# Another order of work in a state-space mixer: quarter-array inputs, transposes over the outputs' bank, weight groups held to ready tiles

## The chip, the cores and the metric

The kernel runs on one core of a Trainium2 chip. Its engines work side by side, each through its own instructions in order: TensorE (PE) multiplies matrices, VectorE (DVE) and ScalarE (ACT) do elementwise work, GpSimd (POOL) does some more and starts DMAs, and SyncE's queue (SP) starts most of the DMAs. The metric is the device time of one execution, in microseconds (us); lower is better.

## The reference, cut to what matters

The program is one step of a decoder with two layers. Layer 0 mixes tokens with a short convolution, layer 1 with a complex diagonal state-space model and a gated output. Each layer ends in a squared-ReLU MLP. There are 272 prompt positions and 32 sample positions, held as 304 columns (four interleaved rows of 76), and 2048 features, which are 16 tiles of 128.

```python
def s5_mixer(u, h0_re, h0_im, ...):          # layer 1; 128 groups of 16 channels, 64 complex states each
    abar, bbar = discretise(lam, log_step, b)
    bu = einsum('btgc,gpc->btgp', u32, bbar)               # inputs of the states
    h = scan(h_t = abar * h_{t-1} + bu_t)                  # over positions, with the initial state h0
    y = einsum(c, h) + d_skip * u32
    g = gelu(y)
    return (g @ w_a) * sigmoid(g @ w_b)                    # 2048 x 2048 each
...
h = h + mixer(rmsnorm(h)); h = h + sq_relu_mlp(rmsnorm(h), w_up, w_down)    # 2048 -> 8192 -> 2048
```

## The kernel before, in words

**Weights and slots.** Every weight matrix is read as pieces of 256 rows by 512 columns (512 KB), one piece to a *slot*. ACT rounds a piece to its high half `whi` (L67), DVE subtracts to get the low half `wlo` (L69), and PE makes 24 products per slot (L200 to L202: high by high, high by low, low by high, for four blocks of 128 outputs and two feature tiles). `take()` of slot i prepares the halves of slot i+2 and starts DMAs some slots further ahead. Halves lie in three buffers, so the halves of slot i+2 need slot i-1 to be finished. A *group* is a run of slots that sum into four PSUM banks of seven that go round; the next group's fourth bank is the first of the group before, so it must have been read by then.

**Layer 0's MLP and the work behind it.** Up groups (8 slots) and down groups (4 slots each, four in a row) alternate. Results of an up group are taken out one per slot during the next group, in a chain across DVE and ACT: `zt` (L919), `at` (L921), high half on ACT (L814), low half on DVE (L815). Results of a down group are added to `h` (L876). Meanwhile a list `bg` of small jobs computes the mixer's matrices (powers of the decay, input and output matrices, rotations); after every slot the next job, or the next piece of a job that contains `yield`, is emitted. The jobs that the change touches are `t_a4` and `t_a4b` (transposes on PE and copies on DVE), `t_m2` (output matrices: a product, a second product, their sum, on DVE, L680 to L683) and `t_rot` (rotation tables).

**The mixer.** For each of the 16 feature tiles t:

- `st_m1` (L1036): the inputs of the states, from `ssm["U"]` by a matrix `m1` that DMAs load from DRAM. A tile's two halves of 64 channels stand as blocks on the diagonal of a 128 x 128 matrix whose other blocks are zero, written once by `G.memset` and then left. Two matrices are held. The result lies in PSUM banks 4 and 5 (`xbank`).
- `st_scan` (L1064 to L1076) on DVE: two products by the rotation and their sum, `scale_u` (L1180) for tile t+2, the scan (L1069), two products back, the states `S` and the last state. On ACT `st_samples` (L1051, L1052) copies the sample columns and `rho_fill` (L1056) writes decays.
- `st_t` (L1098) and `st_y` (L1108) on PE: outputs from the inputs and from the states, in half arrays, into banks 6 and 7 (`ybank`); ACT copies them out (L1114).
- `st_c(t)`: PE transposes the outputs (L1121) into `cbank`, unused columns of banks 4 and 5; ACT does the gelu (L1123) and the high half of `g` (L1125); the low half, `lo()` (L1128), runs on DVE.

**What fills the PE between them.** The gated output's weights are multiplied as early as `g` allows: `EARLY` lists groups and how many feature tiles each takes before the loop ends (partial sums are copied out by ACT, L1209, and added later), `LATE` lists what is left. `PERSTEP[t]` says how many slots step t may emit, half of them at `between(1)`, the rest at `between(2)`, and `run_slots` emits a slot only when the tiles that it needs are past `lo()`. In steps 0 and 1 ten matmuls of ones by ones (`warm`, L1225) follow `st_t`. The order of every engine is the order in which this code runs; nothing reorders it.

**Names of steps used below.** "Step t" is one pass of the loop over tiles. y(t) stands for the output matmuls L1108 of tile t, m1(t) for its input matmuls.

Of the kernel before, what the change touches and what calls it, by code (L numbers as in the profile page):

```python
# [31 lines left out]
WARM = 10  # L32
ULAG = 2
WP = 12
# [46 lines left out]
def build(ctx, tc, I, O, dbg=None):  # L81
# [369 lines left out]
    def prep_tasks():  # L451
# [112 lines left out]
        def t_a4():  # L564
# [38 lines left out]
        def t_a4b():  # L603
            ps = psum1()
            for x, n in enumerate((27, 0, 1)):
                T.transpose(out=ps[:64, x * P:(x + 1) * P], in_=nat(n), identity=ident)
            for g2 in range(2):
# [61 lines left out]
        def t_m2(ri, hf, i):  # L669
# [12 lines left out]
            V.tensor_tensor(out=tmp, in0=c[1 - ri], in1=a[1], op=ALU.mult)  # L682
            V.tensor_tensor(out=o, in0=o, in1=tmp, op=ALU.add if ri == 0 else ALU.subtract)  # L683
# [105 lines left out]
        L += [None] * 12  # L789
        for c in range(8):  # L790
            L.append(lambda c=c: t_kmm(c))
            if c < 6:
                L.append(lambda c=c: t_kload(c + 2))
            L += [lambda c=c: t_rot(c), lambda c=c: t_rotout(c)]
# [157 lines left out]
    def ssm_alloc():  # L952
# [3 lines left out]
        ssm["m1"] = [xr[:, i * 1024:(i + 1) * 1024].rearrange("p (n m) -> p n m", m=P) for i in range(2)]  # L956
        ssm["m2"] = [xr[:, 2048 + i * 512:2560 + i * 512].rearrange("p (n m) -> p n m", m=64) for i in range(2)]
        ssm["tt"] = [xr[:, 3072 + i * 256:3328 + i * 256].rearrange("p (n m) -> p n m", m=64) for i in range(2)]
        ssm["rot"] = [xr[:, 3584 + i * 816:3584 + (i + 1) * 816] for i in range(3)]
        ssm["tmp"] = [xr[:, 6032 + i * 544:6032 + (i + 1) * 544] for i in range(3)]  # L960
        ssm["yt"] = [xr[:NK, 7664 + i * 512:8176 + i * 512] for i in range(2)]
        sel = ssm["sel"] = xr[:, 8688:9200].rearrange("p (j m) -> p j m", j=4)
# [9 lines left out]
        G.memset(xr[:, 0:2048], 0.0)  # L972
# [5 lines left out]
        for t in range(2):  # L978
            load_m1(t)
            load_rot(t)  # L980
        load_rot(2)
        for t in range(2):
            load_t(t)
            load_m2(t)
        ssm["h0"] = b[:, 0:1024].rearrange("p (r a x) -> p r a x", r=2, a=4)
# [24 lines left out]
    def load_m1(t):  # L1010
        for g2, g in enumerate(HALF):
            nc.sync.dma_start(out=ssm["m1"][t % 2][g, :, g], in_=d_m1[t, g2].rearrange("x q r p -> x (q r) p"))

    def load_m2(t):
        nc.sync.dma_start(out=ssm["m2"][t % 2], in_=d_m2[t].rearrange("g x q r p -> (g x) (q r) p"))
# [9 lines left out]
    xbank = banks[:, 2048:3072].rearrange("p (q x) -> p q x", q=4)  # L1025
    xst = xbank[:, :, 0:2 * NK].rearrange("p q (r k) -> p q r k", r=2)
    ybank = [banks[:NK, 3072 + g * 512:3328 + g * 512] for g in range(2)]
    cbank = xbank[:, :, 2 * NK:3 * NK]
    GBANK = (0, 1, 2, 3)

    def st_m1(t):

        m = ssm["m1"][t % 2]
# [4 lines left out]
        if t + 2 < NT:  # L1038
            load_m1(t + 2)
# [8 lines left out]
    def st_samples(t):  # L1048

        qs = slice(t * 4, t * 4 + 4)  # L1050
        S.activation(out=ssm["F0"][:, 1:9, :, qs].rearrange("p s r q -> p q r s"), in_=xst[:, :, :, NP:NK], func=AF.Copy)  # L1051
# [7 lines left out]
    def st_scan(t, between):  # L1059
# [3 lines left out]
        x = xst[:, :, :, 0:NP]  # L1063
        V.tensor_tensor(out=v3(a), in0=x, in1=co, op=ALU.mult)  # L1064
        V.tensor_tensor(out=v3(b), in0=x[:, :, ::-1], in1=si, op=ALU.mult)
        between(0)
        V.tensor_tensor(out=a, in0=a, in1=b, op=ALU.add)
        between(1)
        V.tensor_tensor_scan(out=b, data0=ssm["rho"][t % 2], data1=a, initial=0.0, op0=ALU.mult, op1=ALU.add)  # L1069
        between(2)  # L1070
        V.tensor_tensor(out=v3(a), in0=v3(b), in1=co, op=ALU.mult)
        V.tensor_tensor(out=v3(c), in0=v3(b)[:, :, ::-1], in1=si, op=ALU.mult)
        between(3)
# [29 lines left out]
    def st_y(t):  # L1103

        for n in range(8):
            q, r = n // 2, n % 2
            for g2, g in enumerate(HALF):
                T.matmul(out=ybank[g2][:, q * 64:(q + 1) * 64], lhsT=ssm["S"][t % 2][g, q, r, :], rhs=ssm["m2"][t % 2][g, n, :],  # L1108
                         start=False, stop=n == 7)
        if t + 2 < NT:  # L1110
            load_m2(t + 2)
# [27 lines left out]
    def warm_sqrt():  # L1139
        w = tp.tile([P, 1], F32, tag="warm", name="warm")  # L1140
        S.activation(out=w, in_=one1, func=AF.Sqrt)
# [4 lines left out]
    def ssm_pre(t):  # L1146
        def sa():
# [4 lines left out]
            if t == 5:  # L1152
                warm_sqrt()
# [10 lines left out]
    flush()  # L1164
    u_in(8, NT)
# [7 lines left out]
    rsqrt_from(ps[:, :NK], rstd2[:, NK:2 * NK], rstd2[:, 2 * NK:3 * NK], rT)  # L1173
    for f in h0_copies:
        f()
# [14 lines left out]
    def early():  # L1190

        for (n, mg), c in EARLY:
# [7 lines left out]
            for si in range(0, c, 2):  # L1200
                yield si + 2
                hi, lo = W.take()
                for m, kk in slot_order(si, si + 2 >= c):
                    mm(m, kk, si, hi, lo)
            for i in range(4):
                if (n, mg) in pslot:
                    a = pslot[n, mg] * 4 + i
# [170 lines left out]
```

## Time and profile before

| what | value |
|---|---|
| median of 3 runs | 2521.21 us (2519.66 to 2521.39) |
| profiled execution | 2520.97 us, span 2519.0 us |
| PE busy | 2438.4 us, 97% of the span |
| DVE busy | 1537.7 us, 61% |
| ACT busy | 965.3 us, 38% |
| POOL busy | 134.6 us, 5% |
| the mixer | from about 1360 us of the span to about 1560 us |

The page counts busy time per engine, but matmuls are pipelined, so a busy PE is not always at full speed; the granted clock (full is 2.4 GHz, shown as 1.00; 0.50 is 1.2 GHz) has to be read beside it. A wait is put down to the semaphore that came last. Where a row shows `x16`, so many instructions that follow each other are merged, and an fp32 matmul counts as two.

### The profile page before, as it was taken

How to read it: one execution, taken by the hardware profiler on the slowest of the kernel's cores; microseconds unless marked ns; L12 is line 12 of the kernel's file. 1: busy time of each engine (PE TensorE's matmuls, PEld its weight loads, DVE VectorE, ACT ScalarE, POOL GpSimd, SP SyncE). 2: the span in 40 equal slices, each digit the busy share in tenths (PEclk: the TensorE clock that was granted, in tenths of full speed). 3: DMA queues.
4: the chain of work that ended last, by engine and by line, in shares of the span. 5: the costliest groups of instructions: out<-in, count | busy, mean ns of one | idle time of the engine just before them, and what ended most of it. 6: DMA issues, size and time to landing. Idle time of an engine off the chain costs nothing.

```text
span 2519.0 us, 44232 instructions
## 1 busy us (share of the span) xinstructions
PE 2438.4 (97%) x18526; PEld 2418.0 (96%) x18526; DVE 1537.7 (61%) x2302; ACT 965.3 (38%) x1241; POOL 134.6 (5%) x239
## 2 busy tenths in 40 slices
PE   6999999999999999999998898999999999999998
PEld 6999999999999999999998898999999999999997
DVE  5644555875657774767655776676555555545555
ACT  4333334434433333333433443453333333333334
POOL 2000000000011120000300002000000000000000
PEclk9999999999999999999998899999999999999999
DMA  6555555456676667666759663556555555555553
GB/s 153 157 159 157 157 158 178 143 150 185 162 214 174 195 189 211 195 202 208 214 161 228 167 189 121 170 165 166 165 166 167 168 161 169 165 168 167 167 165 109
DMA packets 245829, 432.39 MB, mean 172 GB/s; under 512 B 48404, under 2 KB 52180, under 8 KB 245596
## 3 DMA queue, kind: packets, MB, share of 16 engines
q1 hardware_dynamic: 236160, 396.30, 53.9%
q0 software_dynamic: 9408, 33.20, 5.3%
q8 instruction: 145, 2.38, 0.4%
q14 instruction: 56, 0.46, 0.1%
q10 hardware_dynamic: 60, 0.05, 0.0%
HBM read 400.44 MB, written 29.05 MB: 171 GB/s over the span
## 4 chain that ended last, share of the span: by engine, by line
PE 51%; DMA 1%; ACT 1%; issue 0%; DVE 0%; SPq 0%; DVEq 0%; ACTq 0%
PE banks L200 16%; PE banks L202 16%; PE banks L201 16%; PE banks L1036 1%; PE banks L1108 1%; DMA d_u<-h 1%; PE banks L1098 0%; DMA ssm_xr<-d_m 0%; PE banks L1342 0%; SPq L1006 0%; ACT gt L1123 0%; PE banks L1225 0%; PE banks L1121 0%; ACT sq L324 0%; ACT ssm_big L1209 0%
## 5 line engine op out<-in xcount | busy, mean ns | idle before, releaser
L69 DVE TENSOR_TENSOR wlo<-raw,whi 128x1024 fp32r<-128x1024 f32 x704 | 864.2, 1228 | 810.7 <-ACT whi L67 809.6
L67 ACT ACTIVATE whi<-raw 128x1024 fp32r<-128x1024 f32 x704 | 742.7, 1057 | 956.0 <-PE banks L201 806.0
L200 PE MATMUL banks<-hid,whi 128*128 128x304 f32 (+1 forms) x2048 | 611.9, 299 | 15.6 <-DVE h L876 13.8
L202 PE MATMUL banks<-xs_m,wlo 128*128 128x304 f32 (+1 forms) x2048 | 611.8, 299 | 0.7 <-DVE wlo L69 0.7
L202 PE MATMUL banks<-hid,wlo 128*128 128x304 f32 (+1 forms) x2048 | 611.1, 298 | 1.3 <-DVE wlo L69 1.3
L201 PE MATMUL banks<-hid,whi 128*128 128x304 f32 (+1 forms) x2048 | 611.7, 299 | 0.0
L201 PE MATMUL banks<-xs_m,whi 128*128 128x304 f32 (+1 forms) x2048 | 611.0, 298 | 0.0
L200 PE MATMUL banks<-xs_m,whi 128*128 128x304 f32 (+1 forms) x2048 | 610.8, 298 | 0.0
L200 PEld LDWEIGHTS banks<-hid,whi 128*128 128x128 f32 x2048 | 385.7, 188 | 17.8 <-DVE h L876 15.3
L202 PEld LDWEIGHTS banks<-hid,wlo 128*128 128x128 f32 x2048 | 386.5, 189 | 2.1 <-DVE wlo L69 2.1
L202 PEld LDWEIGHTS banks<-xs_m,wlo 128*128 128x128 f32 x2048 | 385.4, 188 | 1.6 <-DVE wlo L69 1.6
L200 PEld LDWEIGHTS banks<-xs_m,whi 128*128 128x128 f32 x2048 | 385.3, 188 | 1.3 <-issue 0.4
L201 PEld LDWEIGHTS banks<-hid,whi 128*128 128x128 f32 x2048 | 385.8, 188 | 0.0
L201 PEld LDWEIGHTS banks<-xs_m,whi 128*128 128x128 f32 x2048 | 385.3, 188 | 0.1
L200 PE MATMUL banks<-xs,whi 128*128 128x304 f32 x768 | 233.6, 304 | 3.6 <-DVE h L391 3.6
L202 PE MATMUL banks<-xs,wlo 128*128 128x304 f32 x768 | 233.3, 304 | 0.0
L201 PE MATMUL banks<-xs,whi 128*128 128x304 f32 x768 | 232.6, 303 | 0.0
L814 ACT ACTIVATE hid<-at 128x304 fp32r<-128x304 f32 (+1 forms) x128 | 57.8, 452 | 302.2 <-DVE at L921 302.2
L200 PE MATMUL banks<-g,whi 128*128 128x288 f32 x512 | 154.8, 302 | 0.7 <-ACT g L1125 0.7
L201 PE MATMUL banks<-g,whi 128*128 128x288 f32 x512 | 151.9, 297 | 0.9 <-DVE g L1128 0.9
L202 PE MATMUL banks<-g,wlo 128*128 128x288 f32 x512 | 151.7, 296 | 0.0
L200 PEld LDWEIGHTS banks<-xs,whi 128*128 128x128 f32 x768 | 145.8, 190 | 3.9 <-DVE h L391 3.8
(260 smaller groups left out, 2304.3 us busy)
## 6 DMA issues: line engine op xcount, KB each, us to landing
raw<-in_mlp_w_up SPq DMA_DIRECT2D x256, 512.0 KB, 3.8
raw<-in_mlp_w_down SPq DMA_DIRECT2D x256, 512.0 KB, 3.8
raw<-in_conv_w_in SPq DMA_DIRECT2D x96, 512.0 KB, 3.8
raw<-in_conv_w_out SPq DMA_DIRECT2D x32, 512.0 KB, 3.7
raw<-in_ssm_glu_w_a SPq DMA_DIRECT2D x32, 512.0 KB, 3.7
raw<-in_ssm_glu_w_b SPq DMA_DIRECT2D x32, 512.0 KB, 4.2
d_rot<-prep POOLq DMA_DIRECT2D x8, 816.0 KB, 4.3
ssm_xr<-d_rot SPq DMA_DIRECT2D x16, 408.0 KB, 4.7
```

The lines of the kernel that those rows point to most:

```text
L67: self.nc.scalar.activation(out=hi, in_=r, func=AF.Copy)
L69: eng.tensor_tensor(out=lo, in0=r, in1=hi.bitcast(F32), op=ALU.subtract)
L200: T.matmul(out=o, lhsT=wh, rhs=xh, start=si == 0 and kk == 0, stop=False)
L201: T.matmul(out=o, lhsT=wh, rhs=xl, start=False, stop=False)
L202: T.matmul(out=o, lhsT=wl, rhs=xh, start=False, stop=si + 2 >= len(kts) and kk == 1)
L814: S.activation(out=dh, in_=src, func=AF.Copy)
L1036: T.matmul(out=xbank[:, q, r * NK:(r + 1) * NK], lhsT=m[:, q * 2 + r, :], rhs=ssm["U"][:, t * 4 + q, :], start=True, stop=True)
L1108: T.matmul(out=ybank[g2][:, q * 64:(q + 1) * 64], lhsT=ssm["S"][t % 2][g, q, r, :], rhs=ssm["m2"][t % 2][g, n, :], start=False, stop=n == 7)
```

## The change

1. **Inputs by quarters of the array.** `m1` matrices are held as 128 x 64 (the two diagonal blocks below each other), four buffers instead of two, one DMA each instead of two. `st_m1` issues for each of 8 outputs two matmuls, of rows and columns 0 to 63 and of rows and columns 64 to 127. The zero fill is gone. Tile 1's inputs go to banks 2 and 3 and tiles 0, 2 and later to banks 4 and 5, so that tiles 0 and 1 are issued before the loop. `m2` has three buffers instead of two.
2. **Transposes over the outputs' accumulator.** `cbank` is now bank 6, the first of the two that `st_t` and `st_y` sum into.
3. **Order of a step.** `PERSTEP` holds two numbers: slots before `st_c(t-1)` and slots after the scan. `st_samples` comes after the transposes and the gelu of the tile before, `st_m1(t+1)` at `between(0)`, `st_t` at the end of the step. Before the second slots, `W.prep_to` prepares halves ahead of `lo()`.
4. **Gated groups.** `EARLY` starts with b0 and holds 18 slots; `LATE` ends with a whole group a3 of 8 slots. The first late group (7 slots) is emitted by the same generator as the early ones, with the same test on ready tiles. Its slots are ordered so that the earlier of two feature tiles goes first.
5. **Warm-up and tables.** `warm` is gone except for six matmuls in step 1; seven come before the sum of squares, fifteen instead of twelve after it; the activation table for gelu is loaded before the loop.
6. **Background jobs.** `t_a4` issues its four matmuls together and yields before the copies and once more after them; `t_a4b` yields after its transposes; `t_m2` yields between its second product and the sum; the first two rotations stand in place of twelve empty entries and the others one tile earlier.

```diff
-EARLY = [(("a", 0), 2), (("b", 1), 2), (("a", 1), 2), (("b", 2), 4), (("a", 2), 6), (("b", 3), 8), (("a", 3), 10),
-         (("b", 0), 16)]
-LATE = [(n, c) for n, c in EARLY[:-1]]
-PERSTEP = (0, 0, 1, 1, 2, 2, 1, 2, 1, 2, 2, 2, 2, 2, 2, 2)
+EARLY = [(("b", 0), 2), (("a", 0), 2), (("b", 1), 2), (("a", 1), 4), (("b", 2), 6), (("a", 2), 8), (("b", 3), 12)]
+LATE = EARLY + [(("a", 3), 0)]
+PERSTEP = ((0, 0), (0, 0), (0, 1), (1, 1), (1, 1), (1, 1), (0, 1), (1, 1), (1, 1), (1, 1), (1, 1), (1, 0), (0, 1),
+           (1, 1), (1, 1), (1, 0))
...
             for x in range(4):
+                T.matmul(out=ps[32 * x:32 * x + 16, 256:256 + P], lhsT=nat(30, 16), rhs=ident, start=True, stop=True)
+            yield
+            for x in range(4):
                 sl = slice(32 * x, 32 * x + 16)
-                T.matmul(out=ps[sl, 256:256 + P], lhsT=nat(30, 16), rhs=ident, start=True, stop=True)
...
             V.tensor_tensor(out=tmp, in0=c[1 - ri], in1=a[1], op=ALU.mult)
+            yield
             V.tensor_tensor(out=o, in0=o, in1=tmp, op=ALU.add if ri == 0 else ALU.subtract)
...
-    xbank = banks[:, 2048:3072].rearrange("p (q x) -> p q x", q=4)
-    cbank = xbank[:, :, 2 * NK:3 * NK]
+    xbank = [banks[:, o:o + 1024].rearrange("p (q x) -> p q x", q=4) for o in (2048, 1024)]
+    cbank = banks[:, 3072:3072 + N0].rearrange("p (i k) -> p i k", i=4)
...
         for q in range(4):
             for r in range(2):
-                T.matmul(out=xbank[:, q, r * NK:(r + 1) * NK], lhsT=m[:, q * 2 + r, :], rhs=ssm["U"][:, t * 4 + q, :],
-                         start=True, stop=True)
+                for g in HALF:
+                    T.matmul(out=x[g, q, r, :], lhsT=m[g, q * 2 + r, :], rhs=ssm["U"][g, t * 4 + q, :],
+                             start=True, stop=True)
...
     for t in range(NT):
-        n = PERSTEP[t]
+        na, nb = PERSTEP[t]
+        run_slots(na)
+        low = st_c(t - 1) if t else None
         def between(k):
             if k == 0:
-                st_samples(t)
-            elif k == 1:
                 if t + 2 < NT:
                     scale_u(t + 2)
-                k = run_slots((n + 1) // 2)
-                if t > 2:
-                    lows.append(st_c(t - 1))
-                if t + 1 < NT:
+                if t == 0:
+                    st_m1(2)
+                elif 1 < t < NT - 1:
                     st_m1(t + 1)
-                st_t(t)
-                warm(WARM if t < 2 else 0)
-            elif k == 2:
-                run_slots(n // 2)
+            else:
+                W.prep_to(W.idx + nb * (LOOK + 1))
+                if low:
+                    low()
+                run_slots(nb)
         st_scan(t, between)
+        st_t(t)
+        if t == 1:
+            warm_pe0(6)
         st_y(t)
+    run_slots(1)
+    low = st_c(NT - 1)
+    run_slots(1)
+    low()
+    run_slots(9)
```

**Where instructions move.** The first place is PE at the start of the mixer, up to the first slot. Before:

```order
L993 MATMUL banks<-ident,ssm_big 128x128 x8
L1170 MATMUL banks<-acc,ssm_xr 128x76 x4
L263 MATMUL banks<-ones 128x128 x12
L1036 MATMUL banks<-ssm_big,ssm_xr 128x76 x16
L1098 MATMUL banks<-ssm_xr,ssm_big 76x64 x8
L1225 MATMUL banks<-ones 128x128 x10
L1108 MATMUL banks<-ssm_xr,vy 76x64 x16
L1121 MATMUL banks<-ident,ssm_xr 128x76 x4
L1036 MATMUL banks<-ssm_big,ssm_xr 128x76 x8
```

Then tile 1's L1098, L1225, L1108 and L1121 follow in the same way, and the first slot. In the changed kernel the same jobs have the lines L1004, L1185, L1051 (inputs), L1112 (`st_t`), L1122 (y), L1135 (transposes) and L1239 (the six matmuls of ones):

```order
L1004 MATMUL banks<-ident,ssm_big 128x128 x8
L263 MATMUL banks<-ones 128x128 x7
L1185 MATMUL banks<-acc,ssm_xr 128x76 x4
L263 MATMUL banks<-ones 128x128 x15
L1051 MATMUL banks<-ssm_big,ssm_xr 64x76 x48
L1112 MATMUL banks<-ssm_xr,ssm_big 76x64 x8
L1122 MATMUL banks<-ssm_xr,vy 76x64 x16
L1135 MATMUL banks<-ident,ssm_xr 128x76 x4
L1112 MATMUL banks<-ssm_xr,ssm_big 76x64 x8
L1239 MATMUL banks<-ones 128x128 x6
L1122 MATMUL banks<-ssm_xr,vy 76x64 x16
```

The inputs of tiles 0, 1 and 2 (48 quarter matmuls) now stand together ahead of everything, and ten of ones are gone from each of steps 0 and 1, with six back in step 1.

The second place is ACT in one step late in the loop. Before, from y's copies (L1114) on, with the sample copies L1051 and L1052 and the gelu L1123:

```order
L1114 ACTIVATE ssm_xr<-banks 76x16x16 x2
L1051 ACTIVATE ssm_big<-banks 128x4x2x8
L1052 ACTIVATE vy<-ssm_big 128x8x8
L67 ACTIVATE whi<-raw 128x1024
L1123 ACTIVATE gt<-banks 128x288
L1125 ACTIVATE g_13689<-gt 128x288
```

In the changed kernel, with L1128 for y's copies, L1137 and L1139 for gelu and high half, L1066 and L1067 for the sample copies:

```order
L1128 ACTIVATE ssm_xr<-banks 76x16x16 x2
L67 ACTIVATE whi<-raw 128x1024
L1137 ACTIVATE gt<-banks 128x288
L1139 ACTIVATE g_13722<-gt 128x288
L1066 ACTIVATE ssm_big<-banks 128x4x2x8
L1067 ACTIVATE vy<-ssm_big 128x8x8
```

The sample copies moved from ahead of the gelu to behind it, and the inputs of the next tile (L1051 on PE), which overwrite the bank that L1066 reads, wait for L1066.

The third place is DVE in layer 0's MLP, at the end of the first down group after an up group. Before, with L680 (product), L682 and L683 (second product and sum) of the job `t_m2`:

```order
L69 TENSOR_TENSOR wlo<-raw,whi 128x1024
L919 TENSOR_TENSOR zt<-banks,rstd 128x304
L921 SCALAR_TENSOR_TENSOR at<-zt 128x304
L815 TENSOR_TENSOR hid<-at,hid 128x304
L680 TENSOR_TENSOR prep_7178<-prep_7178,nat 128x32x16
L69 TENSOR_TENSOR wlo<-raw,whi 128x1024
L682 TENSOR_TENSOR prep_7178<-prep_7178,nat 128x512
L683 TENSOR_TENSOR prep_7178<-prep_7178 128x32x16
L876 TENSOR_TENSOR h<-h,banks 128x304
```

The same rows of the changed kernel, where L928, L930, L824 and L885 are L919, L921, L815 and L876:

```order
L69 TENSOR_TENSOR wlo<-raw,whi 128x1024
L928 TENSOR_TENSOR zt<-banks,rstd 128x304
L930 SCALAR_TENSOR_TENSOR at<-zt 128x304
L824 TENSOR_TENSOR hid<-at,hid 128x304
L69 TENSOR_TENSOR wlo<-raw,whi 128x1024
L885 TENSOR_TENSOR h<-h,banks 128x304
```

In these four slots the background work on DVE went from four products and two sums, with two operations more before the first L876, to one product and one sum, with none before L885. One such down group later it is five operations (L684, L686, L688, L684, L686) in place of eight.

## Rows read from the trace of the kernel before

**Rows 1.** The page: busy time, share and instructions by engine
```profile
PE 2438.4 (97%) x18526; PEld 2418.0 (96%) x18526; DVE 1537.7 (61%) x2302; ACT 965.3 (38%) x1241; POOL 134.6 (5%) x239
```
**Rows 2.** Waits of PE up to 1345 us: total, times, longest
```profile
PE banks L572 <- DVE nat L573: 4.3, 3, 3.8
...
PE banks L202 <- DVE wlo L69: 2.0, 4, 1.0
PE banks L200 <- DVE zt L919: 1.8, 1, 1.8
```
**Rows 3.** Windows: length, busy of PE, PEld, DVE, ACT, POOL, clock, DMA, GB/s
```profile
507.00:518.00 11.00, 6.65 (x29) 4.83 (x27) 7.30 (x25) 2.35 (x3) 0.00 (x0) 0.69 0.43 105
800.00:950.00 150.00, 139.03 (x972) 137.81 (x971) 110.18 (x135) 50.60 (x56) 20.07 (x27) 0.98 0.65 195
```
**Rows 4.** Timeline of PE, layer 0's down groups: start, length, [idle before, releaser]
```profile
823.45 0.41 PE L200 MATMUL banks<-hid,whi 128*128 128x304 f32 x1 [3.94 <-DVE h L876]
...
936.32 0.41 PE L200 MATMUL banks<-hid,whi 128*128 128x304 f32 x1 [3.95 <-DVE h L876]
```
**Rows 5.** Timeline of DVE in the down group before 823 us
```profile
802.95 1.23 DVE L69 TENSOR_TENSOR wlo<-raw,whi 128x1024 fp32r<-128x1024 f32 x1 [7.05 <-ACT whi L67]
...
806.54 1.23 DVE L69 TENSOR_TENSOR wlo<-raw,whi 128x1024 fp32r<-128x1024 f32 x1 [0.47 <-ACT whi L67]
...
810.61 1.20 DVE L69 TENSOR_TENSOR wlo<-raw,whi 128x1024 fp32r<-128x1024 f32 x1
...
815.75 1.22 DVE L69 TENSOR_TENSOR wlo<-raw,whi 128x1024 fp32r<-128x1024 f32 x1
```
**Rows 6.** Chain of work that ended last, one step: start, length, work
```profile
1509.23 0.69 PE banks L1098 x16
...
1513.29 1.24 PE banks L1108 x32
...
1517.91 0.28 PE banks L1121 x4
...
1518.67 2.01 PE banks L1036 x16
```
**Rows 7.** The same chain, the mixer's start
```profile
1381.73 7.36 DMA ssm_xr<-d_m
1389.23 3.66 PE banks L1036 x16
...
1394.10 4.39 PE banks L1225 x20
...
1408.93 1.31 PE banks L1108 x32
```
**Rows 8.** Timeline of DVE, first and last operation of tile 0's scan
```profile
1369.64 0.72 DVE L1064 TENSOR_TENSOR ssm_xr<-banks,ssm_xr 128x544 f32<-128x544 f32 x1 [2.48 <-PE banks L1036]
...
1375.41 0.17 DVE L1076 TENSOR_TENSOR ssm_big<-ssm_xr 128x8 f32<-128x8 f32 x1
```
**Rows 9.** Timeline of ACT in one step of the mixer
```profile
1526.02 0.65 ACT L1114 ACTIVATE ssm_xr<-banks 76x256 f32<-76x256 f32 x2 [5.43 <-PE banks L1108]
1526.56 0.31 ACT L1051 ACTIVATE ssm_big<-banks 128x64 f32<-128x64 f32 x1
...
1526.90 1.06 ACT L67 ACTIVATE whi<-raw 128x1024 fp32r<-128x1024 f32 x1
...
1530.12 0.44 ACT L1125 ACTIVATE g<-gt 128x288 fp32r<-128x288 f32 x1
```
**Rows 10.** Chain of work, matmuls of a background job in quarter columns
```profile
1184.31 0.69 PE banks L730 x32
```
**Rows 11.** Timeline of DVE, the scan of the last tile
```profile
1541.55 2.35 DVE L1069 TENSOR_TENSOR_SCAN ssm_xr<-vy,ssm_xr 128x544 f32<-128x544 f32 x1
```
**Rows 12.** Chain of work, outputs of the last tile
```profile
1550.32 2.31 PE banks L1108 x32
```
**Rows 13.** Timeline of ACT, last copy of the 25th slot's sums
```profile
1559.88 0.41 ACT L1211 ACTIVATE vy<-banks 128x288 f32<-128x288 f32 x1 [0.39 <-PE banks L202]
```

More of the change, by code (lines that the diff above doesn't have):

```diff
@@ L1010, in load_m1 @@
     def load_m1(t):
[L1011 to L1012 removed]
+        nc.sync.dma_start(out=ssm["m1"][t % 4], in_=d_m1[t].rearrange("g x q r p -> (g x) (q r) p"))
     def load_m2(t):
[L1015 removed]
+        nc.sync.dma_start(out=ssm["m2"][t % 3], in_=d_m2[t].rearrange("g x q r p -> (g x) (q r) p"))
     def load_t(t):
@@ L1107, in st_y @@
             for g2, g in enumerate(HALF):
-                T.matmul(out=ybank[g2][:, q * 64:(q + 1) * 64], lhsT=ssm["S"][t % 2][g, q, r, :], rhs=ssm["m2"][t % 2][g, n, :],
+                T.matmul(out=ybank[g2][:, q * 64:(q + 1) * 64], lhsT=ssm["S"][t % 2][g, q, r, :], rhs=ssm["m2"][t % 3][g, n, :],
                          start=False, stop=n == 7)
-        if t + 2 < NT:
-            load_m2(t + 2)
+        if t + 3 < NT:
+            load_m2(t + 3)
         y = ssm["yt"][t % 2].rearrange("k (i q g e) -> k g i q e", i=4, q=4, g=2)
@@ L1202, in early, with warm_pe0 @@
                 hi, lo = W.take()
-                for m, kk in slot_order(si, si + 2 >= c):
+                for m, kk in [(m, kk) for m in range(4) for kk in range(2)] if c == 2 else slot_order(1, False):
                     mm(m, kk, si, hi, lo)
             for i in range(4):
-                if (n, mg) in pslot:
-                    a = pslot[n, mg] * 4 + i
-                    assert a < 16 or (a - 15) * N1 <= outs[0] * 4 * NK
-                    S.activation(out=part[:, a, :], in_=ps[i][:, :N1], func=AF.Copy)
-                else:
-                    S.activation(out=ssm["sg"][i], in_=ps[i][:, :N1], func=AF.Sigmoid)
+                a = pslot[n, mg] * 4 + i
+                assert a < 16 or (a - 15) * N1 <= outs[0] * 4 * NK
+                S.activation(out=part[:, a, :], in_=ps[i][:, :N1], func=AF.Copy)
+        kts = KALL[LATE[0][1]:]
+        for _ in range(4):
+            k = GBANK[nbank[0] % 4]
+            nbank[0] += 1
+            first.append(banks[:, k * 512:(k + 1) * 512])
+        mm = products(first, kts, rhs_g, N1)
+        for si in range(0, len(kts), 2):
+            yield kts[si] + 2
+            hi, lo = W.take()
+            for m, kk in slot_order(1, False):
+                mm(m, kk, si, hi, lo)
+    def warm_pe0(n):
+        for _ in range(n):
+            T.matmul(out=banks[:, 0:P], lhsT=ones, rhs=ones, start=True, stop=True)
     outs = [0]
+    first = []
     work = early()
@@ L1221, in run_slots @@
         return n
-    def warm(n):
-        for _ in range(n):
-            T.matmul(out=banks[:, 0:P], lhsT=ones, rhs=ones, start=True, stop=True)
     for t in range(2):
@@ L1293, in ev_ga @@
         sg = ssm["sg"][(mg % 2) * 4 + i]
-        V.tensor_tensor(out=pt, in0=pt, in1=ps[:, :N1], op=ALU.add)
-        V.tensor_tensor(out=sg, in0=sg, in1=pt, op=ALU.mult)
+        if pt is not None:
+            V.tensor_tensor(out=pt, in0=pt, in1=ps[:, :N1], op=ALU.add)
+        V.tensor_tensor(out=sg, in0=sg, in1=ps[:, :N1] if pt is None else pt, op=ALU.mult)
         hv = cols(h[:, t, :], N1)
@@ L1305, in build @@
     for gi, ((n, mg), c) in enumerate(LATE):
-        ps = group(KALL[c:], rhs_g, N1)
+        ps = group(KALL[c:], rhs_g, N1) if gi else first
         for i in range(4):
             f = ev_gb if n == "b" else ev_ga
-            later(lambda f=f, mg=mg, i=i, p=ps[i], pt=part[:, gi * 4 + i, :]: f(mg, i, p, pt), front=True)
+            later(lambda f=f, mg=mg, i=i, p=ps[i], pt=part[:, gi * 4 + i, :] if c else None: f(mg, i, p, pt), front=True)
     fb = {}
```

76 lines of the change are left out of this document (39 added, 37 removed).

## The prediction, written before the run

> **What bounds the kernel now.** I read the page first, then PE's waits by stretch, then windows with the granted clock, and last the chain of waits through the mixer. The page shows PE busy for 97% of the span [rows 1], so the kernel ends when PE has worked through its list: time is gained only where PE idles, runs at half clock, or does work that can go. There are two such places away from the two ends. The first is layer 0's MLP, where background work on DVE delays PE: three waits in `t_a4` [rows 2], and in the stretch from 800 to 950 us 10.97 us of idle PE with a mean clock of 0.98 [rows 3]. The two largest waits there, 3.94 and 3.95 us, are for L876, which frees a PSUM bank at the start of the second down group [rows 4]. The second place is the mixer, read as a chain of work. In a full step the chain runs on PE alone but for one wait, and its start and its end hold long waits [rows 6, 7, 12].
>
> **Change of `t_a4`.** PE waits 4.3 us there [rows 2], because its second matmul waits for a copy that stands behind DVE's other work. In the 11 us from 507 on PE is busy for 6.65 and the clock averages 0.69 [rows 3]: 0.31 of 11 us at half clock means about 6.8 us at half, of which some 5.6 fell on busy PE, so 2.8 us of work were lost. With the matmuls issued together nothing on DVE stands between them, and the copies run a slot later, where nobody on PE waits for them. Term: 4.3 + 2.8 = 7.0 gained (bounds 4.3, if the clock falls anyway, and 7.1).
>
> **Change of `t_m2`.** A slot in which an up group's result is taken out costs DVE and ACT, which hand it back and forth, 806.54 - 802.95 = 3.59 us; with one background operation 810.61 - 806.54 = 4.07; with two 815.75 - 810.61 = 5.14 [rows 5]. PE's slot takes 24 products of 0.14, 3.3 us. Four such slots in a row follow each up group. In the first place, from 802.95 to the end of L876 at 823.4, the chain took 20.45 us. By the new order the four slots hold one operation, one, none and none, and none stands ahead of L885: about 4.7 + 4.07 + 3.59 + 3.59 + 1.6 = 17.5 us, against 13.3 of PE. In the second place the old order gives 5.7 + 4.07 + 5.14 + 4.07 + 3.6 = 22.6 us and a wait of 3.95, so the chain may lag some 5 us before PE notices; the new order gives 19.6. That leaves about 1 us of wait in the second place; in the first the lag of 4.2 is under that slack, and I leave 1 us there too, since the jobs' DMAs now fall into these slots. Of the 10.97 us idle and the 3.0 lost to the clock (150 us by 0.02) [rows 3] that takes 12.0 (bounds 0, if the waits only move, and 14). The jobs end some 63 us later, in down groups of 3.3 us slots with 1.2 + 0.5 + 1.1 us on DVE, which fit. The other shifted jobs (ACT's rounding of the input matrices, their DMAs, the rotations) cause waits of about 1.5 us in four places now; three slots' shift leaves their number as it is, and I cost it at nothing (bounds -3 and +3).
>
> **Price of a quarter matmul.** The trace has no such matmul. The nearest row is a background job whose instructions use 32 columns of the array each, four side by side into one bank: 32 instructions of 80 moving columns in 0.69 us [rows 10]. Two side by side instead of four would be 1.38, and with 76 columns 1.31. The outputs y, two half arrays into two banks, have 32 instructions of 64 columns in 1.24 [rows 6], which scales to 1.47. So m1 falls from 2.01 [rows 6] to about 1.3 us (bounds 0.69, if it is as cheap as rows 10, and 4.0, if each of the 32 costs what each of the 16 costs now).
>
> **Mixer, the start.** Before, y(2) starts at 1408.93 [rows 7]. Tile 0's scan starts at 1369.64 and takes 5.95 us [rows 8]; the warm-up matmuls after it, and in step 1 also the DMA of m1(2), which is queued on SP behind the transfers of U and ends at 1389.1, put off everything [rows 7]. Both go: matrices 0 to 3 are loaded long before. By the new order: three more warm-up matmuls cost 0.65 and the shorter m1(0) gives 0.7 back, so y(0) starts at about 1375.6. DVE goes straight to tile 1: 5.95 and 1.3 for the low half of g and the wait for it, 1382.9; six matmuls of ones at half clock (12 instructions by 0.22 [rows 7], 2.6 us) end at 1383.7. Then y(1) 1.8, copies 0.65, transposes to m1(3) 1.6, m1 1.3; slot 0 needs the low half, which stands behind a weight's rounding 1.06 and subtraction 1.23: it starts at about 1390.6, and 3.3 + 0.69 later comes y(2), at 1394.5. Start: 14.4 gained.
>
> **Mixer, the steps.** Now a step with two slots takes 2.01 + 0.69 + 3.37 + 1.24 + 3.37 + 0.28 and 0.48 of waiting for the gelu, 11.44 (a slot is 1513.29 - 1509.92) [rows 6]. The transposes leave `xbank`, but the wait does not: m1(t+1) overwrites the bank that the sample copy L1066 of tile t reads, and that copy now stands on ACT behind the gelu and the high half. From the transposes' start to m1 it is 0.28 + 0.48 + 0.44 + 0.31, with handoffs 1.6 [rows 6, 9], where it was 0.76. New step on PE: 1.24 + 3.37 + 1.6 + 1.3 + 3.37 + 0.69 = 11.57. What the quarters save, the later copy takes. On DVE the step begins with a weight's subtraction that waits for its rounding, which stands on ACT behind y's copies: 1.24 + 0.65 + 1.06 + 1.23 = 4.18, then the scan's 5.8, a second subtraction and the half of g, less overlaps about 11.4: just hidden. From y(2) to y(15) there are nine steps of 11.6, two with one slot after the scan (1.24 + 0.7 + 1.6 + 1.3 + 3.37 + 0.69 = 8.9), step 11 with one slot before (bound by DVE, 10.6) and step 15, bound by DVE while GpSimd's work on the samples slows it as now (the scan takes 2.35 there against 1.28 [rows 11]; four operations of about +1): 14.1. Sum 146.9, so y(15) starts at 1541.4, against 1550.32 [rows 12], with one slot fewer done.
>
> **Mixer, the end.** Before, the 25th slot ends 9.5 us after y(15) starts [rows 12, 13], nearly all at half clock: y takes 2.31 against 1.24. In the new order y(15), a slot, the transposes and a last slot follow each other without gaps, 8.2 us at full clock; PE has idled about 8 us before, so the first 8.4 us run at half clock, as now, and the end comes after 12.4, at 1553.8. Against 1559.85 the mixer gains 6.0 (bounds: -9 and +16, from m1 between 1.9 and 0.69 over 14 steps and from 4 us more or less at start and end).
>
> **The rest of the gated output.** Slots and products are equal in number. Group b3 has only two slots left, in which three results of a2 have to be taken out: a delay of 0.8 us (bounds 0 and 4). The table load moved off the chain is within the start's sum.
>
> **Sum.** -7.0 - 12.0 - 6.0 + 0.8 = -24.2. The profiled execution took 2520.97 us, 0.24 below the median, so about 2497.
>
> **Rivals.** *Quarters that do not overlap.* Both quarters of an output write one bank. The Trainium skill, TensorEngine Tiling (Array Packing), Restrictions and Gotchas, says that different row tiles cannot access the same PSUM bank at the same time; the two halves of y go to two banks, and rows 10 share a bank but not among row tiles, so no run here decides it. If such pairs run one after the other, m1 is 2.6, 1.3 more in each of 14 steps: +18, 2515. *The waits of layer 0 only move.* If half of the 19 us there stays because other jobs take the place of these in the tight slots, 2506; for it speaks that a plain slot already takes 3.59 against 3.3, against it the counted operations. *DVE becomes the bound of a step.* It is 0.2 below PE by my sum; half a microsecond more in 11 steps gives 2503. *A quarter costs a whole.* On the other side: the 16 instructions of m1 now take 126 ns each, and if that is a cost per instruction, m1 takes 4.0, +2.7 in 14 steps and in the two at the start that lie on the path, +40: 2537. It turns slower where m1 passes 2.9 us. Rows 10, at 22 ns per instruction, speak against it.
>
> **How the numbers follow.** Forecast 54% (own range 2488 to 2507, from the bounds of the parts), waits that move 17%, DVE as the bound 15%, one bank 8%, whole price 6%. The range 2486 to 2515 leaves out the last case and the tails. 0.2%, 5 us, is what can be told from no change. Faster by more: the forecast, the two at 2503 and 2506 and part of the one at 2515, together 0.87 after taking off for their upper tails; within it 0.07; slower 0.06.
>
> **What would show it.** No wait of PE for L575 and a clock of 1.00 from 507 to 518; waits for L885 of about 1 us where 3.9 stood; y(2) about 14 us earlier; m1 near 1.3 us with a wait of about 1.3 for L1066 ahead of it; steps of 11.6; an idle PE of some 8 us before y(15). Wrong it would be made by m1 above 2 us, by steps above 12, or by new waits over 3 us between 550 and 1000 us.

## The result and the profile after

| | time before | time after |
|---|---|---|
| median | 2521.30 us (2519.66 to 2521.44) | 2501.76 us (2499.43 to 2503.56) |
| profiled execution | 2520.97 us, span 2519.0 | 2503.56 us, span 2501.5 |

The ratio is 0.9923, with a 95% interval of 0.9906 to 0.9941. The changed kernel is 20 us faster by the medians. The profiled executions differ by 17.4: the one after is the longest of its four runs.

Read as three stretches of PE's timeline, the difference is this. Layer 0's MLP (up to the transposes that open the mixer) ends at 1345.07 instead of 1359.07, 14.0 earlier. From there to the end of the 25th weight slot the mixer takes 95.6 us instead of 100.8. What follows takes 1.6 longer.

The page's line of busy times, and PE's waits up to 1345 us (total, times, longest; first the row of the kernel before that [rows 2] leave out), answer to [rows 1, 2]:

```profile
PE 2418.4 (97%) x18774; PEld 2399.3 (96%) x18774; DVE 1531.8 (61%) x2302; ACT 966.9 (39%) x1242; POOL 129.9 (5%) x238
```

```profile
PE banks L200 <- DVE h L876: 13.8, 6, 3.9
```

```profile
PE banks L200 <- DVE h L885: 9.3, 6, 2.9
...
PE banks L202 <- DVE wlo L69: 1.2, 3, 0.5
PE banks L609 <- DVE nat L604: 1.1, 1, 1.1
```

PE is busy 20.0 us less with 248 instructions more; m1 has twice as many and is cheaper. The wait in `t_a4` is gone, a small new one of `t_a4b` (L609) is there, and the waits for L885 (L876 before, 13.8 us in 6) still make 9.3.

The two windows of [rows 3] again, with the same columns:

```profile
507.00:518.00 11.00, 11.00 (x86) 10.57 (x85) 9.71 (x25) 4.47 (x5) 0.00 (x0) 1.00 0.60 176
800.00:950.00 150.00, 148.84 (x1073) 148.59 (x1073) 105.25 (x133) 54.85 (x60) 20.10 (x27) 1.00 0.69 203
```

Both stretches came out as full as forecast: the first is all work at full clock, the second idles 1.16 us instead of 10.97. What remains for L885 is elsewhere, in PE's timeline (start, length, then the wait before it and its releaser):

```profile
595.37 0.41 PE L200 MATMUL banks<-hid,whi 128*128 128x304 f32 x1 [2.93 <-DVE h L885]
...
705.54 0.41 PE L200 MATMUL banks<-hid,whi 128*128 128x304 f32 x1 [1.50 <-DVE h L885]
...
721.14 0.41 PE L200 MATMUL banks<-hid,whi 128*128 128x304 f32 x1 [2.03 <-DVE h L885]
...
923.93 0.41 PE L200 MATMUL banks<-hid,whi 128*128 128x304 f32 x1 [1.17 <-DVE h L885]
```

The first three lie in 550 to 800 us, where the jobs on the input matrices run; before, that stretch had two waits of 1.5. ACT's timeline just ahead of the first shows how it arises:

```profile
590.70 2.04 ACT L636 ACTIVATE prep<-prep 128x1024 f32<-128x1024 f32 x1
592.64 1.04 ACT L67 ACTIVATE whi<-raw 128x1024 fp32r<-128x1024 f32 x1
```

A copy of 2.04 us for an input matrix stands ahead of a weight's rounding; DVE's subtraction waits for that, and L885, behind the subtraction, frees PE's bank late.

One full step of the mixer on PE, to be held against [rows 6] (y, transposes, m1, `st_t`; slots left out):

```profile
1437.26 1.31 PE L1122 MATMUL banks<-ssm_xr,vy 64*76 64x64 f32 x32
...
1441.78 0.43 PE L1135 MATMUL banks<-ident,ssm_xr 76*128 76x76 f32 x4
1443.38 1.27 PE L1051 MATMUL banks<-ssm_big,ssm_xr 64*64 64x76 f32 x32 [1.17 <-ACT ssm_big L1066]
...
1448.23 0.76 PE L1112 MATMUL banks<-ssm_xr,ssm_big 64*76 64x64 f32 x16
```

m1 takes 1.27 where it took 2.01, and begins 1.60 after the transposes where it began 0.76 after them. The same step on DVE, its two weight subtractions and the last operation that y waits for:

```profile
1440.19 1.23 DVE L69 TENSOR_TENSOR wlo<-raw,whi 128x1024 fp32r<-128x1024 f32 x1 [2.95 <-ACT whi L67]
...
1444.95 1.20 DVE L69 TENSOR_TENSOR wlo<-raw,whi 128x1024 fp32r<-128x1024 f32 x1
...
1448.45 0.17 DVE L1090 TENSOR_TENSOR ssm_big<-ssm_xr 128x8 f32<-128x8 f32 x1
```

From 1440.19 on DVE works without a gap until y(8) can start at 1448.83. Its only idle time, 2.95, is spent on the rounding, which stands on ACT behind y's copies. So the loop from y over ACT and DVE to the next y looks as long as PE's own order, to some 0.3 us; the experiments on the loops below test that.

The mixer's start on PE, in place of [rows 7], has one wait that I had not counted; its end, in place of [rows 12], has the idle time that I had:

```profile
1380.38 1.03 PE L1112 MATMUL banks<-ssm_xr,ssm_big 64*76 64x64 f32 x15 [2.97 <-DMA ssm_xr<-d_t]
```

```profile
1530.91 2.29 PE L1122 MATMUL banks<-ssm_xr,vy 64*76 64x64 f32 x32 [8.98 <-issue]
```

And the scan of the last tile on DVE with an operation behind it, as in [rows 11], and GpSimd's work at that time:

```profile
1521.97 2.37 DVE L1084 TENSOR_TENSOR_SCAN ssm_xr<-vy,ssm_xr 128x544 f32<-128x544 f32 x1
...
1525.63 1.78 DVE L1086 TENSOR_TENSOR ssm_xr<-ssm_xr 128x544 f32<-128x544 f32 x1
```

```profile
1523.27 2.12 POOL L1103 TENSOR_TENSOR ssm_big<-a,ssm_big 128x512 f32<-128x512 f32 x1
```

### The profile page after: what moved, and what is told of

It reads as the page before. It is cut to its first block, busy times and chain, and to the rows that moved or that the text cites. A ratio compares the mean times of both kernels' runs of the same rounds, so it can differ in the third digit from the quotient of the medians.

```text
span 2501.5 us, 44712 instructions
## 1 busy us (share of the span) xinstructions
PE 2418.4 (97%) x18774; PEld 2399.3 (96%) x18774; DVE 1531.8 (61%) x2302; ACT 966.9 (39%) x1242; POOL 129.9 (5%) x238
## 4 chain that ended last, share of the span: by engine, by line
PE 50%; DMA 1%; ACT 1%; issue 1%; DVE 1%; SPq 0%; ACTq 0%; DVEq 0%
PE banks L200 16%; PE banks L202 16%; PE banks L201 16%; PE banks L1122 1%; DMA d_u<-h 1%; PE banks L1051 1%; PE banks L1369 0%; PE banks L1112 0%; DMA ssm_big<-d_u 0%; DMA ssm_xr<-d_t 0%; ACT gt L1137 0%; ACT g L1139 0%; PE banks L1135 0%; DVE wlo L69 0%; ACT whi L67 0%
```

## The experiments

Times are medians; the ratio is to the kernel before, run on the same chip. The chips differ: the kernel before took 2521.3 to 2524.3 on them, so between two kernels the ratios say more than the medians. Spans of single stretches are from the profiled execution of each kernel. In the kernels with the changed layer 0 its MLP ended anywhere from 1341.4 to 1348.5, so stretches of the mixer are counted from that end. "After MLP" counts from the end of layer 0's MLP, and step t runs from y(t-1) to y(t); y(15) stands at 191.3 there before and at 185.8 in the changed kernel.

**Layer 0 alone, the mixer alone.** The first kernel is the old one with part 6 of the change only (background jobs), the second the changed one without it. Besides the pauses shown further down, that part moves the rotations:

```diff
-        L += [None] * 12
+        L += [lambda: t_rot(0), lambda: t_rotout(0), lambda: t_rot(1), lambda: t_rotout(1)]
```

> The kernel before with nothing but the edits of the background jobs (t_a4, t_a4b, t_m2, the rotations three slots earlier); the mixer is the old one. Theory: the two parts of the change are independent, and layer 0 holds most of it: its MLP ended at 1345.07 instead of 1359.07 us of the span in the changed kernel, so about 14 us less here too, 2507 us, ratio 0.9944; the mixer from the end of the MLP to the end of its 25th slot stays at 100.8 us. Rival: the mixer needs what the jobs write (matrices, rotations), and jobs that end later make the old mixer wait for its transfers; then 3 to 6 us of the 14 come back there and the time is 2510 to 2513.

2507.01 us, ratio 0.9941 (0.9928 to 0.9953). The MLP ends at 1342.9, y(15) follows 190.5 later. The old mixer takes no longer when the jobs end later.

> The changed kernel with the background jobs as they were before; only the mixer and what surrounds it is new. Theory: from the end of layer 0's MLP to the end of the 25th slot the mixer takes 95.7 us instead of 100.8, so 5 us less, 2516 us, ratio 0.998; the MLP ends at 1359 as before, with 3.9 us waits for L876's counterpart. Rival: the start of the mixer gained because the jobs had ended at other times; then the mixer alone gives nothing (ratio 1.000).

2518.97 us, ratio 0.9987 (0.9978 to 0.9996); y(15) at 184.1 after MLP, so the mixer gains by itself. 0.9941 times 0.9987 is 0.9928, the whole change has 0.9923: the two parts add up, some 15 us from layer 0 and 3 from the mixer (1 to 5.5 by the interval).

**The two edits in layer 0, one by one.** The old kernel with this:

```diff
             for x in range(4):
+                T.matmul(out=ps[32 * x:32 * x + 16, 256:256 + P], lhsT=nat(30, 16), rhs=ident, start=True, stop=True)
+            yield
+            for x in range(4):
...
+            yield
             for g2 in range(2):
...
                 T.transpose(out=ps[:64, x * P:(x + 1) * P], in_=nat(n), identity=ident)
+            yield
```

> The kernel before with the edits of t_a4 and t_a4b alone (four matmuls together, copies a slot later, and three pauses more, which move all later jobs by three slots). Prediction: 7.0 us less, 2514, ratio 0.9972; the shifted jobs cost nothing. Theory from the trace after: the shift puts the jobs on the input matrices where PE waits for their slots: 2.9 us near 595 and 2.0 near 720 where 1.5 and 1.5 stood, one of 1.5 more near 705 and 1.1 for the new copies of t_a4b (L609's wait near 533), together some 4 to 5 us back; net 2 to 3 us less, 2519, ratio 0.999.

2522.64 us, ratio 0.9999 (0.9990 to 1.0009): nothing, less than even my second theory. PE's waits from 400 to 1350 us, and three of them in the timeline:

```profile
PE banks L200 <- DVE h L880: 16.2, 7, 4.0
```

```profile
595.16 0.41 PE L200 MATMUL banks<-hid,whi 128*128 128x304 f32 x1 [2.93 <-DVE h L880]
...
929.71 0.62 PE L200 MATMUL banks<-hid,whi 128*128 128x304 f32 x1 [3.96 <-DVE h L880]
...
1267.99 0.41 PE L200 MATMUL banks<-hid,whi 128*128 128x304 f32 x1 [2.51 <-DVE h L880]
```

The stretch from 507 to 518 is full, as in the changed kernel. But all of PE's waits listed between 400 and 1350 sum to 22.9 us here and to 21.9 before: three slots' shift of the later jobs gave back all that `t_a4` had saved, some of it as far away as 1268 us.

```diff
             V.tensor_tensor(out=tmp, in0=c[1 - ri], in1=a[1], op=ALU.mult)
+            yield
             V.tensor_tensor(out=o, in0=o, in1=tmp, op=ALU.add if ri == 0 else ALU.subtract)
```

> The kernel before with nothing but the pause between the second product and the sum of t_m2. Prediction: the two waits of 3.9 us fall to about 1 and with the clock's losses 12 us go: 2509, ratio 0.9952. Theory from the trace after: the same here, since the jobs before t_m2 keep their slots; the waits near 600 and 615 stay at 1.5. Rival (the waits only move, and it takes both edits to lose them): 3.9 turns up in the group after, 4 to 8 us less, ratio 0.997.

2508.42 us, ratio 0.9947 (0.9933 to 0.9962): this one line is worth 13 us, nearly all that layer 0 gave. The window of [rows 3], and one wait that did move, to a place where the kernel before has none and the changed kernel has none either:

```profile
800.00:950.00 150.00, 149.31 (x1076) 149.04 (x1076) 107.38 (x133) 54.63 (x60) 14.90 (x21) 1.00 0.69 204
```

```profile
1255.69 0.62 PE L200 MATMUL banks<-hid,whi 128*128 128x304 f32 x1 [3.45 <-DVE h L877]
```

**What quarters are worth.** The changed kernel with whole-array matmuls, then with the quarters in another order:

```diff
-                for g in HALF:
-                    T.matmul(out=x[g, q, r, :], lhsT=m[g, q * 2 + r, :], rhs=ssm["U"][g, t * 4 + q, :],
-                             start=True, stop=True)
+                n = min(q * 2 + r, 6)
+                T.matmul(out=x[:, q, r, :], lhsT=m[:, n:n + 2, :], rhs=ssm["U"][:, t * 4 + q, :],
+                         start=True, stop=True)
```

> The changed kernel with m1 issued as before, 8 matmuls on the whole array per tile in place of 16 on quarters; the matrix it reads is the 128 x 64 buffer taken 128 columns wide, so the inputs of the states are not the reference's. Theory of the prediction: PE's order sets the length of a step, m1 takes 2.01 instead of 1.27, and of the 0.74 nothing is hidden: 13 steps by 0.74, about 10 us slower than the changed kernel, 2511, ratio 0.996. Rival, from the trace after: a step is bound as tightly by DVE and ACT (y, its copies, the rounding of a weight, the subtraction, the scan) as by PE; then part of the 0.74 falls into slack of under 0.3 us, and it is 6 to 10. Second rival: quarters were worth less, because PE waits for the sample copy anyway: 0.

2515.97 us, ratio 0.9969 (0.9956 to 0.9983), 14 us slower than the changed kernel by the medians and 12 by the ratios: at or above the theories' 10. Its ten executions spread from 2505.6 to 2520.6, and the profiled one, 2518.0, is a long one. Its two-slot steps at full clock take 11.83, 0.46 more than 11.37: the rival's slack of some 0.3 is real. But five steps (6, 7, 12, 13, 14) take 1.9 to 3.7 more, together 11.7. PE's timeline of m1 in step 7, and the window around it (clock third from the end; the changed kernel has 1.00 in this stretch):

```profile
1437.02 2.01 PE L1051 MATMUL banks<-ssm_big,ssm_xr 128*128 128x76 f32 x16 [1.17 <-ACT ssm_big L1066]
```

```profile
1431.00:1445.00 14.00, 12.83 (x141) 12.45 (x138) 8.36 (x12) 4.79 (x10) 0.00 (x0) 0.88 0.53 159
```

In steps 7, 13 and 14, after a wait of 1.17 and a whole m1 of about 2.0 to 2.4, the granted clock is half in most of the next slot; in the changed kernel's two-slot steps from step 4 on, with quarters of 1.27, it stays at 1.00. In steps 6 and 12 it had fallen before m1 ended. With 0.46 off each of the five steps, some 9 of the 14 us that the quarters brought in these two executions were clock. The matrix, which is not the reference's, is not needed for that: the next kernel computes what the reference does, with an m1 of 2.11, and its clock averages 0.87 in six of the eight two-slot steps from step 4 on.

```diff
-        for q in range(4):
-            for r in range(2):
-                for g in HALF:
+        for g in HALF:
+            for q in range(4):
+                for r in range(2):
```

> The changed kernel with the order of the 16 quarter matmuls turned: all 8 of rows 0 to 63 first, then all 8 of rows 64 to 127, so that no two neighbours in the order use different quarters except once. Theory: the 1.27 us of m1 come from two quarters that work side by side, though both write one PSUM bank; one after the other they cost twice as much, 2.3 to 2.6 us. Rival: a quarter matmul is simply cheap (40 ns each of 32 instructions), no overlap at all; then m1 stays at 1.27 us.

One run, 2525.36 us, too few to compare times. m1 at full clock:

```profile
1440.58 2.11 PE L1051 MATMUL banks<-ssm_big,ssm_xr 64*64 64x76 f32 x32 [1.17 <-ACT ssm_big L1066]
```

2.11 / 32 is 66 ns, against 40 when neighbours use different quarters. So instructions of different quarters overlap in part, into one bank (whether it is the multiplications or the loading of one's matrix during the other's, these runs don't tell), and a lone quarter is also cheaper than the whole array's 126 ns (2.01 / 16); I had expected at least 2.3.

**Which loop sets a step.** Three kernels: sample copies early, first rounding early, both (with the second rounding early too).

```diff
+        st_samples(t)
         low = st_c(t - 1) if t else None
```

> The changed kernel with the copies of the samples (L1066, L1067) on ACT ahead of the transposes and the gelu of the tile before, instead of behind them. Theory of the prediction (PE's order sets the step, and what the quarters save goes into the wait for L1066): PE's wait of 1.17 ahead of m1 goes in 12 steps, steps of 10.3 instead of 11.37, about 13 us less, 2488. Rival, from the trace after: the loop y, y's copies, rounding, subtraction, scan, y takes 11.36 as well, so PE only waits elsewhere (ahead of y); the two-slot steps stay at 11.3, only the steps with one slot lose 1.2, in all 2 to 3 us less, 2499, ratio 0.991.

2503.91 us, ratio 0.9922 (0.9905 to 0.9938): no change; the two-slot steps stay, as the rival says. m1's wait shrinks by half, and its step stays at 11.3, because DVE still idles 2.94 for the rounding. The gelu that the row names ends at 1444.92, and DVE's second product, which reads the bank that m1 overwrites, at 1444.97:

```profile
1445.08 1.27 PE L1051 MATMUL banks<-ssm_big,ssm_xr 64*64 64x76 f32 x32 [0.61 <-ACT gt L1136]
```

The 2 to 3 us of the one-slot steps did not come: steps 6 and 12 take 11.46 and 12.36 where the changed kernel has 8.82 and 11.28. In step 6 DVE waits 2.18 for the sample copy, and m1 of tile 7 then runs at half clock (2.29 for 1.27).

```diff
+        if t + 1 < NT and PERSTEP[t + 1][0]:
+            W.hi_to(W.idx + LOOK + 1)
         st_y(t)
```

`hi_to` is the part of `prep_to` that rounds on ACT; the subtraction on DVE keeps its place.

> The changed kernel with the rounding of the next weight piece on ACT (L67, the first of a step) ahead of y's copies instead of behind them; its buffer is free a slot earlier. Theory of two equal loops: DVE's subtraction comes some 2.5 us earlier and the loop through DVE gets slack, but PE's own order with its wait of 1.17 for L1066 still takes 11.3: no change, 0 to 1 us, ratio 0.992. Rival (DVE and ACT alone bind): steps fall to about 10.3, 11 us less, 2490.

2493.98 us, ratio 0.9884 (0.9863 to 0.9905): 8 us less (10 by the ratios), between the theories. The two-slot steps behave as the first says, 11.24 with m1 still waiting 1.16. The gain lies mostly in steps that DVE alone bound: step 11 takes 8.44 instead of 10.25, and step 15 11.52 instead of 15.14, since the scan is over (1520.72) when GpSimd goes on (1521.01). Step 12, behind a PE that idled 0.41 and not 2.17, keeps more of its clock (0.84 instead of 0.70) and takes 10.37 instead of 11.28.

Both edits together, and this one:

```diff
+        W.hi_to(W.idx + nb * (LOOK + 1))
         low = st_c(t - 1) if t else None
```

> The changed kernel with the sample copies ahead of the transposes (as in the run before the last), the first rounding of a step ahead of y's copies (as in the last), and the second one ahead of the gelu. Theory of two equal loops: only with both eased does a step fall, to 1.24 + 3.3 + 0.43 + 1.27 + 3.3 + 0.7, about 10.2 to 10.4; nine two-slot steps by 1.1 and three one-slot steps by 1.2, 12 to 14 us less than the changed kernel, 2488 to 2490, ratio 0.987. Rival (each alone had already what there is to gain): as in the better of the two. Second rival: the gelu, now behind a rounding, comes a microsecond later and the second slot waits for g; then 2 to 6 us less.

2490.07 us, ratio 0.9869 (0.9855 to 0.9884), y(15) at 173.1 after MLP instead of 185.8. PE in one step, transposes, m1, `st_t` and y:

```profile
1447.51 0.43 PE L1144 MATMUL banks<-ident,ssm_xr 76*128 76x76 f32 x4
1447.87 1.27 PE L1061 MATMUL banks<-ssm_big,ssm_xr 64*64 64x76 f32 x32
...
1452.44 0.76 PE L1121 MATMUL banks<-ssm_xr,ssm_big 64*76 64x64 f32 x16
```

No wait is left here and a two-slot step takes 10.0, where each of the two edits alone left it at 11.2 or 11.3: both loops had to be eased, though the early rounding was worth 8 us by itself. What the early second rounding does of this was not tried apart. The start gains nothing: y(3) stands at 50.0 after MLP, in the changed kernel at 49.1.

**GpSimd beside the last scan.**

```diff
-        x, y = (s_.rearrange("p (s q) -> p s q", s=NS) for s_ in ssm["st"])
+        x, y = (ssm["tmp"][i][:, 0:512].rearrange("p (s q) -> p s q", s=NS) for i in (0, 2))
```

> The changed kernel with the two scratch buffers of GpSimd's work on the samples (L1103 to L1106) laid over the scan's own scratch, so that GpSimd can't begin until the last tile's scan is done. Theory: DVE's operations of step 15 take longer because GpSimd runs beside them (the scan 2.37 instead of 1.28, then 1.45, 1.78, 1.78, 1.66 instead of 0.45, 0.72, 0.72, 0.72); alone they take their usual time, y(15) starts 5 us earlier and step 15 takes 10 instead of 15.1; 5 us less, 2497, ratio 0.990. Rival: the last step's DVE operations are slow for another reason (PE's half clock, or the granted rate of that stretch); then nothing changes, and GpSimd's 12 us behind the loop may make the samples' last transposes late. Second rival: the slow-down only moves to the weight subtractions of the next slots, and PE waits there for half of it.

2495.84 us, ratio 0.9893 (0.9878 to 0.9908): 6 us less (8 by the ratios). DVE in step 15, and GpSimd, which now starts behind it:

```profile
1519.27 1.29 DVE L1084 TENSOR_TENSOR_SCAN ssm_xr<-vy,ssm_xr 128x544 f32<-128x544 f32 x1
...
1520.83 0.72 DVE L1086 TENSOR_TENSOR ssm_xr<-ssm_xr 128x544 f32<-128x544 f32 x1
```

```profile
1523.16 1.26 POOL L1103 TENSOR_TENSOR ssm_xr<-a,ssm_big 128x512 f32<-128x512 f32 x1 [275.09 <-DVE ssm_big L1090]
```

Step 15 takes 9.97 instead of 15.14. PE's clock is not what slowed DVE: in the changed kernel it was still 1.00 while the scan took its 2.37, and from 1485 to 1490, at 0.50 and with GpSimd idle, DVE's products took their usual 0.72.

**The transfer at the start.**

```diff
-            nc.sync.dma_start(out=ssm["tt"][t % 2][g],
+            (G if t == 2 else nc.sync).dma_start(out=ssm["tt"][t % 2][g],
```

> The changed kernel with the two transfers of tile 2's output matrix (load_t(2)) issued from GpSimd's queue, which is empty there, instead of SP's, where they stand behind the transfers of U. Theory: PE's wait of 2.97 us ahead of st_t(2) goes, y(2) starts at 33 us from the end of layer 0's MLP instead of 36.1, and PE, without the pause, keeps its full clock through y(2) (1.3 instead of 2.3): 3 to 5 us less in the profile, 2497 to 2499, ratio 0.991. Rival: y(2) then waits for something else of the same time (the rounding of the weight, the DMA of m1 or of the rotation behind the same transfers); then under 1 us.

2497.21 us, ratio 0.9905 (0.9888 to 0.9921); the interval overlaps the changed kernel's. In the trace y(2) starts at 32.5 after MLP (36.1 there), and `st_t(2)` without a wait:

```profile
1373.26 0.76 PE L1112 MATMUL banks<-ssm_xr,ssm_big 64*76 64x64 f32 x16
```

Step 3 falls from 12.96 to 11.37; step 6 loses 1.6 to a fall of the clock. y(15) comes 3.5 earlier.

**All together.** The kernel with both loops eased, with the last two edits added.

> The changed kernel with sample copies and both roundings early, GpSimd's sample work held back behind the last scan, and tile 2's output matrix over the other queue. If the parts add: 2490 of the first, less 4 for step 15 (13.5 us there, which falls to about 9.5) and 3 for the start: 2483, ratio 0.984. Rival (the clock falls at other places once PE has fewer and shorter pauses, or the last step is bound by another chain): 2486 to 2490, ratio 0.986.

2486.22 us, ratio 0.9855 (0.9840 to 0.9870), the fastest version: 15 us under the changed kernel, and within the rival's range. Step 15 takes 8.40 instead of the 13.47 of the kernel with both loops eased. The other queue adds nothing here: y(2) starts at 36.5 after MLP with it, and at 36.6 in the kernel without it, where PE did not wait for that transfer either. In both, DVE's first product in steps 1 and 2 waits for the sample copies (3.2 and 2.2 us). A version with the old place of the copies in the first tiles was not tried.

## Why the prediction was right, point by point

The forecast was 24.2 less in the profiled execution; it was 17.4 there, and 19.5 by the medians. 2501.76 lies in the range, near the upper end of the likeliest case. Most of what is missing is in layer 0, which gained 14.0 of the 19.0 forecast.

- **`t_a4`, 7.0, and the other jobs at nothing (bounds -3 and +3).** This is the step that failed. What it says of the place itself holds: no wait, clock 1.00. But a pause in a list of jobs moves all that follow, and alone the edit gave 0 (ratio 0.9999): if the place gave the 7, the shift cost as much, over twice my bound. In the whole change the waits of 2.93, 1.50 and 2.03 stand where there were two of 1.5, and L609's 1.1 is new.
- **`t_m2`, 12.0 (bounds 0 and 14).** Right: 13 alone, with one wait of 3.45 moved to 1255. The places of [rows 4] wait 0 and 1.17 in the whole change.
- **Price of a quarter, 1.3.** Measured 1.27. The rival on one bank, drawn from the Trainium skill (TensorEngine Tiling (Array Packing), Restrictions and Gotchas), would have given 2.6. The measurement decides: two row tiles of this shape share a bank at 40 ns an instruction, against 66 one after the other (2.11 for m1). The rival of a whole price each is refuted by the same row.
- **The start, 14.4 gained.** 13.7, but by another sum. y(1) came at 22.5 after MLP, 2 us sooner than forecast, and then `st_t(2)` waited 2.97 for a transfer that I had followed for m1 and not for the output matrices. It stood behind the transfers of U before as well (issued at 1385.91), but there PE asked for it only at 1407.80; now PE was ready for it at 1377.4. That the two errors nearly cancel is luck.
- **Steps.** From the transposes to m1 1.60, forecast 1.6. Two-slot steps 11.3 to 11.6 (11.57), step 6 8.82 (8.9), step 11 10.25 (10.6). Too short were step 3 (12.96, the rounding stands behind a late y(2)), step 12 (11.28 for 8.9, after a fall of the clock) and step 15 (15.14 for 14.1). In all 149.7 for 146.9. The kernel before took 141.4 from y(2) to y(15), with one slot more, so the mixer's gain is the start's alone. With whole-array matmuls in the new order y(15) stood at 200.3 after MLP, later than the 191.3 before. Parts 2 to 4 of the change were not tried apart.
- **The end.** 9.8 from y(15) on instead of 12.4: the clock came back while the first slot ran. The mixer gained 5.1, forecast 6.0; that this comes so close is in part luck, because the steps' 2.8 too many and the end's 2.6 too few cancel.
- **The rest, 0.8 lost.** One wait of 0.95 right behind b3, in a3's first slot, as expected; the stretch as a whole lost 1.6.

Of the rivals, *the waits of layer 0 only move* holds for `t_a4`, and for `t_m2` only in the one wait at 1255. *DVE as the bound* is half true: steps are not longer for it, but PE could not have been faster, as the early copies showed, which halved PE's visible wait and brought nothing. Two sums of the prediction are slightly off: 4.3 + 2.8 is 7.1, and 2.7 in 16 places is 43, not 40; no reading hangs on them.

## What to carry to other kernels

A pause put into a list of jobs moves every later job: count what lands in the tight slots, or the gain comes back far away as waits of another name. In a loop over several engines, time each closed chain before easing a wait; with two of equal length the wait on the page is worth nothing alone. When work moves earlier, follow every transfer that it needs, not just the one that was waited for before.

## What the runs showed of the hardware

- **DVE beside GpSimd.** Operations of 128x544 with both inputs in SBUF go from 0.72 to 1.78 while GpSimd adds and multiplies, 1.06 more each; those with one input in PSUM keep 0.71. DVE and GpSimd in the kernel with the first rounding early:

```profile
1515.31 2.06 DVE L79 TENSOR_TENSOR wlo<-raw,whi 128x1024 fp32r<-128x1024 f32 x1 [0.86 <-ACT whi L68]
1517.29 0.71 DVE L1089 TENSOR_TENSOR ssm_xr<-banks,ssm_xr 128x544 f32<-128x544 f32 x1
...
1521.08 1.79 DVE L1096 TENSOR_TENSOR ssm_xr<-ssm_xr 128x544 f32<-128x544 f32 x1
```

```profile
1516.37 2.15 POOL L1115 TENSOR_TENSOR ssm_big<-ssm_big 128x512 f32<-128x512 f32 x1
```

  L1089 runs inside GpSimd's 2.15 us and takes its usual time. The Trainium skill (SBUF — State Buffer, SBUF: two separate sides) says that the two engines share a pair of ports which one of them holds for a whole instruction, and that DVE needs it where it has two SBUF inputs; the trace agrees.
- **Clock.** With the same wait of 1.17 us in each step, the two-slot steps of the changed kernel from step 4 on keep a granted clock of 1.00 behind 1.27 us of quarter matmuls; behind 2.01 of whole ones some fall (0.88 over 14 us) and some do not (1.00 from 1445 to 1480); behind 2.11 of grouped quarters six of eight fall (0.87 over the step). What the engine did before each fall can be read; why one step falls and the next not, these runs do not settle.
